# Two attentions in one block: score order, unit order, where the bias is built, and how operands are evacuated

## The chip, the cores and the metric

The kernel runs on one core of one Trainium2 chip. The metric is the device time of one execution in microseconds. A core has TensorE (matmuls, written PE in the profile; its weight loads are a row of their own, PEld), VectorE (DVE), ScalarE (ACT), GpSimd (POOL) and SyncE (SP), from whose queue the DMA transfers are issued.

## The reference, cut to what matters

Two transformer blocks run one after the other on 256 rows of 1024 numbers. The change lies in the first one, which has two attentions side by side:

```python
h = rmsnorm(x, attn_norm_g)
qa, ka, va, qb, kb, vb = split(h @ w_in)            # 512, 128, 128, 512, 512, 512 columns
# grouped: 8 query heads share 2 key heads of 64 columns
qa, ka = apply_axial_rope(rmsnorm(qa, g)), apply_axial_rope(rmsnorm(ka, g))
out_a = softmax(qa @ ka.T / 8) @ va
# differential: 4 heads, each with two score maps (c = 0, 1) of 64 columns, and a bias by distance
s = rmsnorm(qb, g) @ rmsnorm(kb, g).T / 8 + rel_bias[bucket(k - q)]
p = softmax(s)
out_b = rmsnorm((p[c=0] - lam * p[c=1]) @ vb) * 0.8 * g
x = x + concat(out_a, out_b) @ w_out
x = x + square(relu(rmsnorm(x, mlp_norm_g) @ w_up)) @ w_down
```

Everything is float32. The second block (two gated feed-forward layers, an mLSTM, a forgetting attention) is untouched.

## The kernel before, in words

**Weights and operands.** Weights stream through `Stream` (lines 84 to 147): seven raw buffers are loaded ahead from the SP queue (line 108 or 110), then each load is split into two fp32r halves, `hi` by ScalarE (line 133) and the residual `lo` by an engine named per load, VectorE unless a set in `cdef` says GpSimd (line 134). Six pairs of halves can be alive. A product is three matmuls (lines 251 to 253: hi by hi, hi by lo, lo by hi). The activations' own halves come from `gained` (lines 422 to 432) or `to_hl`: TensorE transposes, ScalarE evacuates the high half, VectorE the residual.

**Order.** The program is written in one order, and the framework (`schedule_with_timeline_sim=True`) deals the instructions out to the engines' queues with that order as priority and a clock of its own, so the order on an engine can differ from the program. Each engine then runs its queue in order.

**The opening.** `opening` (lines 322 to 347) computes keys and values of the grouped attention and its queries for both row tiles, with the weights of eight loads; `rope` and `head_norm` follow on VectorE and ScalarE. Accumulators come from three banks (`acc`), everything else from four (`aux`) and from an eighth bank, `flex`, which every fifth `aux()` takes until the differential attention begins.

**The bias.** Line 609 multiplies the bias table by a one-hot matrix, four fp32 matmuls of 32 rows and 512 columns ahead of the opening in the program. Lines 612 and 614 evacuate them, line 617 stores them to DRAM with a pitch of 513, and line 880, behind the opening, reads them back with a pitch of 512, so that each row is shifted by one.

**The units.** After the opening come twelve units: eight grouped ones (row tile, pair of heads, key head) and then four differential ones (row tile, pair of heads). Each has three stages: `scores`, `trans` (TensorE transposes the exponentials), `pvs`. A loop of 14 passes runs the scores of unit i, the transposes of unit i-1 and the products of unit i-2, then one `fill()`. A fill is the next half chunk of the projections kb, qb, vb (four each), or the next block of the output projection (`wout_q`, two for each row tile and each half of its rows), which is queued when the unit that completes its operand is done. `have` draws fills at once where a unit needs a projection that isn't there yet. In a score matmul the contraction has 64 rows, so it uses one half of the array's 128 rows: key head 0 the lower half, key head 1 the upper; for the differential units map c = 0 the lower and c = 1 the upper. Before, one grouped unit's two matmuls lie on one half. An fp32 matmul shows as two records in the trace.

**The end of the block.** `ev_wo` adds to x and calls `gained` for the next layer's operand, whose `opening` starts the MLP.

## Time and profile before

| what | value |
|---|---|
| median of three runs | 1053.79 us (1047.0 to 1056.36) |
| the profiled execution | 1052.49 us |
| its span, first to last instruction | 1050.7 us |
| mean granted TensorE clock | 0.983 of 2.4 GHz |
| moved by DMA | 212.21 MB, 202 GB/s on average |

The profile is of one execution. Times in the trace count from the span's start. A timeline row gives start and length in us, then engine, line, operation, output and inputs, shapes and how many instructions were merged; in brackets stands how long the engine had been idle and what ended that. A table by stretches gives each engine's busy time in a stretch, the granted clock (1.00 is 2.4 GHz, 0.50 is 1.2 GHz), the share of the DMA engines that was taken and GB/s.

### The profile page before, as it was taken

To read this page: it belongs to the slowest core of one execution; us is meant where nothing else is said; L and a number is where in the kernel's file an instruction comes from. 1 tells how busy PE (TensorE), PEld (TensorE's weight loads), DVE (VectorE), ACT (ScalarE), POOL (GpSimd) and SP (SyncE) were. 2 spreads that over 40 slices of the span, in tenths; PEclk is the share of its full clock that TensorE was granted. 3 is DMA by queue.
4 is the path that set the end of the run, shared out by engine and by line. 5 is a ranking of instruction groups with operands and counts; after the bars stand their busy time and mean duration, and the time that the engine had idled before them with its cause. 6 is when DMAs were issued, how large, how long until landed. Compare 5 with 4: busy or idle time off the path is not lost.

```text
span 1050.7 us, 15208 instructions
## 1 busy us (share of the span) xinstructions
PE 1016.8 (97%) x5861; PEld 870.4 (83%) x5861; DVE 721.6 (69%) x1009; ACT 513.3 (49%) x803; POOL 41.4 (4%) x45
## 2 busy tenths in 40 slices
PE   8899899999999999999999989999999989999998
PEld 5678678998888899998879767787788868999987
DVE  5866657889675565668767889875669776665652
ACT  5567457554453455445434645343464535445540
POOL 1131000000000000000010000000010000000000
PEclk7989999999999999999999999999999999999999
DMA  8734237888884566679817577665456545664741
GB/s 305 235 120 143 79 109 248 272 280 272 314 280 145 181 201 200 183 244 371 284 58 225 179 238 240 205 193 158 134 188 209 201 140 183 218 230 152 263 158 41
DMA packets 104651, 212.21 MB, mean 202 GB/s; under 512 B 7933, under 2 KB 14937, under 8 KB 104578
## 3 DMA queue, kind: packets, MB, share of 16 engines
q1 hardware_dynamic: 104578, 211.24, 60.9%
q8 instruction: 46, 0.75, 0.3%
q14 instruction: 27, 0.22, 0.1%
HBM read 209.11 MB, written 2.10 MB: 201 GB/s over the span
## 4 chain that ended last, share of the span: by engine, by line
PE 71%; DVE 12%; DMA 9%; issue 4%; ACT 2%; SPq 0%; POOL 0%; DVEq 0%; ACTq 0%
PE acc L251 13%; PE acc L252 13%; PE acc L253 12%; DMA raw<-in_w_ada_dram 9%; DVE lo L134 7%; PE acc L312 3%; PE flex L251 3%; PE acc L313 3%; PE flex L253 3%; PE acc L311 3%; PE flex L252 3%; PE flex L311 1%; PE flex L312 1%; PE flex L313 1%; PE aux L375 1%
## 5 line engine op out<-in xcount | busy, mean ns | idle before, releaser
L134 DVE TENSOR_TENSOR lo<-raw,hi 128x1024 fp32r<-128x1024 f32 (+1 forms) x290 | 340.3, 1196 | 68.7 <-ACT hi L133 67.1
L133 ACT ACTIVATE hi<-raw 128x1024 fp32r<-128x1024 f32 (+1 forms) x297 | 301.6, 1027 | 136.7 <-PE acc L253 52.3
L312 PE MATMUL acc<-X,lo 128*128 128x256 f32 x624 | 175.6, 281 | 1.5 <-DVE lo L134 1.5
L311 PE MATMUL acc<-X,hi 128*128 128x256 f32 x624 | 175.8, 282 | 0.0
L313 PE MATMUL acc<-X,hi 128*128 128x256 f32 x624 | 175.4, 281 | 0.0
L472 DVE SCALAR_TENSOR_TENSOR mod<-raw,sc,mod 128x1024 f32<-128x1024 f32 x72 | 92.7, 1288 | 108.3 <-DMA raw<-in_w_ada_dram 108.0
L251 PE MATMUL acc<-hi,X 128*128 128x512 f32 (+1 forms) x320 | 130.7, 410 | 10.8 <-DVE z L1246 4.1
L253 PE MATMUL acc<-hi,X 128*128 128x512 f32 (+1 forms) x320 | 127.5, 401 | 1.2 <-DVE X L380 1.2
L252 PE MATMUL acc<-lo,X 128*128 128x512 f32 (+1 forms) x320 | 127.7, 401 | 0.9 <-DVE lo L134 0.9
L312 PEld LDWEIGHTS acc<-X,lo 128*128 128x128 f32 x624 | 118.2, 189 | 2.1 <-DVE lo L134 1.9
L311 PEld LDWEIGHTS acc<-X,hi 128*128 128x128 f32 x624 | 118.3, 190 | 0.2
L313 PEld LDWEIGHTS acc<-X,hi 128*128 128x128 f32 x624 | 118.1, 189 | 0.3
L251 PEld LDWEIGHTS acc<-hi,X 128*128 128x128 f32 x320 | 61.8, 194 | 30.1 <-DVE z L1246 5.0
L253 PEld LDWEIGHTS acc<-hi,X 128*128 128x128 f32 x320 | 61.8, 193 | 17.8 <-DVE X L432 1.9
L252 PEld LDWEIGHTS acc<-lo,X 128*128 128x128 f32 x320 | 62.0, 194 | 13.6 <-DVE lo L134 1.5
L252 PE MATMUL acc<-lo,U 128*128 128x512 f32 x174 | 68.3, 394 | 1.1 <-DVE lo L134 1.1
L253 PE MATMUL acc<-hi,U 128*128 128x512 f32 x174 | 68.4, 395 | 0.0
L251 PE MATMUL acc<-hi,U 128*128 128x512 f32 x174 | 68.0, 395 | 0.0
L311 PE MATMUL flex<-X,hi 128*128 128x256 f32 x208 | 58.6, 281 | 0.0
L312 PE MATMUL flex<-X,lo 128*128 128x256 f32 x208 | 58.5, 281 | 0.0
L313 PE MATMUL flex<-X,hi 128*128 128x256 f32 x208 | 58.5, 281 | 0.0
L252 PEld LDWEIGHTS acc<-lo,U 128*128 128x128 f32 x174 | 32.7, 188 | 9.1 <-DVE lo L134 1.4
(427 smaller groups left out, 1705.1 us busy)
## 6 DMA issues: line engine op xcount, KB each, us to landing
raw<-in_ffn_w_in_dram SPq DMA_DIRECT2D x80, 512.0 KB, 4.9
raw<-in_w_ada_dram SPq DMA_DIRECT2D x72, 512.0 KB, 4.8
raw<-in_w_mix_dram SPq DMA_DIRECT2D x64, 512.0 KB, 4.5
raw<-in_ffn_w_out_dram SPq DMA_DIRECT2D x44, 512.0 KB, 5.8
raw<-in_w_up_dram SPq DMA_DIRECT2D x32, 512.0 KB, 4.8
raw<-in_w_down_dram SPq DMA_DIRECT2D x32, 512.0 KB, 5.5
raw<-in_w_in_dram SPq DMA_DIRECT2D x16, 512.0 KB, 5.6
raw<-in_w_out_dram SPq DMA_DIRECT2D x16, 512.0 KB, 3.6
```

The lines of the kernel that those rows point to most:

```text
L133: nc.scalar.activation(hi[:, :, :n], r[:, :, :n], AF.Copy)
L134: getattr(nc, eng).tensor_tensor(lo[:, :, :n], r[:, :, :n], hi[:, :, :n].bitcast(F32), ALU.subtract)
L251: nc.tensor.matmul(ps[:, c0:n], h, hi[:, j, c0:n], start=f, stop=False)
L252: nc.tensor.matmul(ps[:, c0:n], h, lo[:, j, c0:n], start=False, stop=False)
L253: nc.tensor.matmul(ps[:, c0:n], l, hi[:, j, c0:n], start=False, stop=z)
L311: nc.tensor.matmul(ps, h, xh, start=first, stop=False, skip_group_check=True)
L312: nc.tensor.matmul(ps, l, xh, start=False, stop=False, skip_group_check=True)
L313: nc.tensor.matmul(ps, h, xl, start=False, stop=last, skip_group_check=True)
L375: nc.tensor.transpose(ps[:, b * P : (b + 1) * P], src[:, b * P : (b + 1) * P], ident)
L472: nc.vector.scalar_tensor_tensor(v, r.rearrange("p a c -> p (a c)"), sc[:, k : k + 1], v, ALU.mult, ALU.add)
```

## The change

Six things change, all in the first block:

- `gained`: VectorE multiplies all 512 columns of a bank by the gain into an SBUF tile, ScalarE copies that as the high half, VectorE subtracts for the residual. Before, each engine did this in four pieces of 128 columns.
- The projections qb and vb no longer name GpSimd for their residuals; VectorE makes all of them.
- The bias is built behind the opening. The table is cut into three bf16 parts stacked on 96 rows, and the one-hot matrix is bf16, three times, so that one bf16 matmul of 96 rows per head replaces the fp32 one. Store and reload keep their form; the reload is issued after the first two fills.
- A grouped pair (key heads 0 and 1) issues its four score matmuls together, in turns between the halves of the array, when its first unit is reached; the second unit finds its bank filled. A differential unit issues its four in turns between the maps.
- The units run as four grouped ones, then differential and grouped in turns: d0, g4, d1, g5, d2, g6, d3, g7.
- `wout_q` starts an accumulator with whichever half of the rows comes first, since for the second row tile that is now the differential one.

```diff
     onehot[bucket, np.arange(512)] = 1.0
+    onehot = np.concatenate([(onehot.view(np.uint32) >> 16).astype(np.uint16).view(np.float32)] * 3, axis=0)
...
     def gained(t, half, g, X):
...
-        for b in range(4):
-            v, gain = ps[:, b * P : (b + 1) * P], cols[:, g + 4 * half + b : g + 4 * half + b + 1]
-            nc.scalar.activation(dh[:, b], v, AF.Identity, bias=0.0, scale=gain)
-            nc.vector.scalar_tensor_tensor(dl[:, b], v, gain, dh[:, b].bitcast(F32), ALU.mult, ALU.subtract)
+        v = s512("xg").rearrange("p (b q) -> p b q", b=4)
+        gain = cols[:, g + 4 * half : g + 4 * half + 4].unsqueeze(2).to_broadcast([P, 4, P])
+        nc.vector.tensor_tensor(v, ps.rearrange("p (b q) -> p b q", b=4), gain, ALU.mult)
+        nc.scalar.activation(dh, v, AF.Copy)
+        nc.vector.tensor_tensor(dl, v, dh.bitcast(F32), ALU.subtract)
...
-        "kava": (512, 256, ()), "qa": (0, 512, ()), "kb": (1280, 512, ()), "qb": (768, 512, (0, 1, 2, 3)),
-        "vb": (1792, 512, (1, 2, 3)),
+        "kava": (512, 256, ()), "qa": (0, 512, ()), "kb": (1280, 512, ()), "qb": (768, 512, ()),
+        "vb": (1792, 512, ()),
...
-    oh = s512("oh")[:32]
-    nc.sync.dma_start(oh, a["onehot"])
...
         def scores(u):
             qt, jp, g = u
...
-            ps = aux()
-            for i in range(2):
-                nc.tensor.matmul(
-                    ps[:, i * S : (i + 1) * S], qaT[g * 64 : (g + 1) * 64, 2 * jp + i, qt * P : (qt + 1) * P],
-                    kaT[g * 64 : (g + 1) * 64, :], start=True, stop=True,
-                )
+            if g == 0:
+                for w in range(2):
+                    sc2[w] = aux()
+                for i in range(2):
+                    for w in range(2):
+                        nc.tensor.matmul(
+                            sc2[w][:, i * S : (i + 1) * S], qaT[w * 64 : (w + 1) * 64, 2 * jp + i, qt * P : (qt + 1) * P],
+                            kaT[w * 64 : (w + 1) * 64, :], start=True, stop=True,
+                        )
+            ps = sc2.pop(g)
...
-            for c in range(2):
-                ps = aux()
-                for i in range(2):
-                    h = 2 * hp + i
+            pss = [aux(), aux()]
+            for i in range(2):
+                h = 2 * hp + i
+                for c in range(2):
                     nc.tensor.matmul(
-                        ps[:, i * S : (i + 1) * S], qbT[c * 64 : (c + 1) * 64, h, qt * P : (qt + 1) * P],
+                        pss[c][:, i * S : (i + 1) * S], qbT[c * 64 : (c + 1) * 64, h, qt * P : (qt + 1) * P],
                         kbT[c * 64 : (c + 1) * 64, h, :], start=True, stop=True,
                     )
+            for c in range(2):
+                ps = pss[c]
...
     opening(xv, it_c["kava"], 256, ev_kava, it_c["qa"], 512, ev_qa)
-    for qt in range(2):
-        o = 255 - P * qt
-        nc.sync.dma_start(bias[:, :, qt, :], tr[:, :, o : o + S])
+    oh = ph.tile([96, S], F32, name="oh")
+    nc.sync.dma_start(oh, a["onehot"])
+    rbp, rbb, rbr = ph.tile([96, 4], BF16, name="rbp"), ph.tile([32, 4], BF16, name="rbb"), ph.tile([32, 4], F32, name="rbr")
+    nc.vector.tensor_copy(rbp[0:32], rb)
+    nc.vector.tensor_tensor(rbr, rb, rbp[0:32], ALU.subtract)
+    nc.vector.tensor_copy(rbb, rbr)
+    nc.vector.tensor_copy(rbp[32:64], rbb)
+    nc.vector.tensor_tensor(rbr, rbr, rbb, ALU.subtract)
+    nc.vector.tensor_copy(rbp[64:96], rbr)
+    bias = bigt([P, 4, 2, S], F32, "bias")
+    for h in range(4):
+        psb = aux()
+        nc.tensor.matmul(psb, rbp[:, h : h + 1].to_broadcast([96, P]), oh.bitcast(BF16), start=True, stop=True)
...
     def wout_q(t, kh):
         for n in range(2):
-            if kh == 0:
+            first = (n, t) not in wo_ps
+            if first:
                 wo_ps[n, t] = acc()
             st.need(it_wo[kh][n])
-            block(wo_ps[n, t], *mv, 4 * kh, it_wo[kh][n], t, 512, kh == 0, kh == 1)
-            if kh == 1:
+            block(wo_ps[n, t], *mv, 4 * kh, it_wo[kh][n], t, 512, first, not first)
+            if not first:
...
-    units = [(gqa_stages, u, (), 0) for u in gqa_units] + [(diff_stages, u, ("kb", "qb"), 1) for u in diff_units]
+    ga_, df_ = [(gqa_stages, u, (), 0) for u in gqa_units], [(diff_stages, u, ("kb", "qb"), 1) for u in diff_units]
+    units = ga_[:4] + [v for pair in zip(df_, ga_[4:]) for v in pair]
...
     fill(2)
     flush()
+    for qt in range(2):
+        o = 255 - P * qt
+        nc.sync.dma_start(bias[:, :, qt, :], tr[:, :, o : o + S])
```

## Rows read from the trace of the kernel before

**Rows 1.** Page: busy us, share of span, instructions.

```profile
PE 1016.8 (97%) x5861; PEld 870.4 (83%) x5861; DVE 721.6 (69%) x1009; ACT 513.3 (49%) x803; POOL 41.4 (4%) x45
```

**Rows 2.** Stretches: length; busy us (instructions) per engine; PEclk; DMA share; GB/s.

```profile
9.00:23.00 14.00, 13.86 (x34) 7.99 (x34) 8.91 (x24) 8.27 (x22) 0.55 (x1) 0.53 1.02 376
...
45.00:57.00 12.00, 7.29 (x28) 4.19 (x27) 9.10 (x28) 6.65 (x20) 0.00 (x0) 0.68 0.14 46
57.00:122.70 65.70, 65.69 (x354) 51.97 (x352) 43.64 (x78) 41.67 (x90) 12.67 (x5) 0.98 0.42 137
122.70:131.20 8.50, 4.12 (x18) 3.63 (x19) 5.17 (x12) 3.85 (x11) 1.02 (x1) 0.80 0.00 0
131.20:153.00 21.80, 20.08 (x94) 15.15 (x93) 10.01 (x20) 10.02 (x21) 2.00 (x3) 1.00 0.24 76
153.00:372.00 219.00, 218.64 (x1296) 192.56 (x1295) 159.42 (x173) 116.19 (x158) 3.00 (x4) 1.00 0.73 246
```

**Rows 3.** Stretches, line 609 alone: PE, PEld, PEclk, DMA share, GB/s.

```profile
9.00:23.00 14.00, 5.69 (x6) 1.49 (x6) 0.53 1.02 376
23.00:45.00 22.00, 1.12 (x2) 0.29 (x2) 1.00 0.95 285
```

**Rows 4.** TensorE's timeline: grouped units (761) alone, a differential unit (824).

```profile
54.64 2.07 PE L761 MATMUL aux<-kaT,qaT 64*128 64x256 f32 x4
...
64.79 1.13 PE L761 MATMUL aux<-kaT,qaT 64*128 64x256 f32 x4
...
106.09 1.14 PE L824 MATMUL aux<-kbT,qbT 64*128 64x256 f32 x8
```

**Rows 5.** One microsecond in which the clock rises; columns as rows 2.

```profile
22.00:23.00 1.00, 1.00 (x3) 0.19 (x1) 0.00 (x0) 0.27 (x1) 0.00 (x0) 0.98 1.06 389
```

**Rows 6.** SP queue, 0 to 60 us, and landing times of the loads.

```profile
4.94 4.15 SPq L110 DMA_DIRECT2D raw<-in_w_in_dram  x6
...
DMA to landing us min/median/max: 5.2/5.5/7.0
```

**Rows 7.** ScalarE's timeline: the seventh load's split.

```profile
25.99 1.06 ACT L133 ACTIVATE hi<-raw 128x1024 fp32r<-128x1024 f32 x1 [2.15 <-issue]
```

**Rows 8.** SP queue: the bias stored and read back.

```profile
24.96 0.37 SPq L617 DMA_DIRECT2D toep<-bias  x1
...
33.96 0.92 SPq L880 DMA_DIRECT2D bias<-toep  x2
```

**Rows 9.** VectorE and GpSimd timelines, 33 to 46 us; GpSimd's splits to 165 us.

```profile
33.52 0.29 DVE L673 TENSOR_TENSOR m<-kn,rc 128x128 f32<-128x128 f32 x1
...
37.75 1.23 DVE L134 TENSOR_TENSOR lo<-raw,hi 128x1024 fp32r<-128x1024 f32 x1
...
39.61 2.13 DVE L673 TENSOR_TENSOR m<-kn,rc 128x128 f32<-128x128 f32 x1
41.66 2.55 DVE L679 TENSOR_TENSOR m<-kn,rs 128x64 f32<-128x64 f32 x2
...
39.19 4.80 POOL L134 TENSOR_TENSOR lo<-raw,hi 128x1024 fp32r<-128x1024 f32 x2 [27.26 <-ACT hi L133]
...
L134 POOL TENSOR_TENSOR lo<-raw,hi 128x1024 fp32r<-128x1024 f32 x7 | 17.5, 2515 | 56.4 <-ACT hi L133 56.2
```

**Rows 10.** Chain of waits, 100 to 132 us: start, length, what.

```profile
118.58 2.09 ACT s L836 x8
...
122.03 1.20 DVE s L829 x2
123.23 1.19 DVE nm L833 x2
```

**Rows 11.** TensorE's timeline in the tail.

```profile
127.08 0.66 PE L375 MATMUL aux<-ident,ob 128*128 128x128 f32 x4 [4.40 <-DVE ob L451]
```

**Rows 12.** Groups to 165 us: busy us, mean ns; the rest is idle time.

```profile
L431 ACT ACTIVATE X<-aux,cols 128x128 fp32r<-128x128 f32 x28 | 9.2, 362 | 4.0 <-DVE X L432 2.5 <-PE aux L427 1.5
L432 DVE SCALAR_TENSOR_TENSOR X<-aux,cols,X 128x128 fp32r<-128x128 f32 x28 | 9.0, 344 | 3.0 <-ACT X L431 2.9
```

More of the change, by code (lines that the diff above doesn't have):

```diff
@@ L603, in body @@
         nc.vector.tensor_scalar(e1[:, t : t + 1], v, EPS, None, ALU.mult)
-    bias = bigt([P, 4, 2, S], F32, "bias")
-    for h in range(4):
-        psb = aux()
-        nc.tensor.matmul(psb, rb[:, h : h + 1].to_broadcast([32, P]), oh, start=True, stop=True)
-        v = bias[:, h].rearrange("p t k -> p (t k)")
-        if h % 2:
-            nc.vector.tensor_copy(v, psb)
-        else:
-            nc.scalar.activation(v, psb, AF.Copy)
-    pitch = 512
-    toep = dram.tile([4, P * (pitch + 1)], F32, name="toep")
-    nc.sync.dma_start(toep.rearrange("h (p j) -> p h j", j=pitch + 1)[:, :, :512], bias.rearrange("p h t k -> p h (t k)"))
-    tr = toep[:, : P * pitch].rearrange("h (p j) -> p h j", j=pitch)
     gq8 = const.tile([P, 9], F32, name="gq8")
@@ L752, in gqa @@
     def gqa():
-        pv, rec, ex, exT = {}, {}, {}, {}
+        pv, rec, ex, exT, sc2 = {}, {}, {}, {}, {}
         def scores(u):
@@ L877, in body @@
     opening(xv, it_c["kava"], 256, ev_kava, it_c["qa"], 512, ev_qa)
-    for qt in range(2):
-        o = 255 - P * qt
-        nc.sync.dma_start(bias[:, :, qt, :], tr[:, :, o : o + S])
+    oh = ph.tile([96, S], F32, name="oh")
[11 more added lines that the diff above has]
+        nc.tensor.matmul(psb, rbp[:, h : h + 1].to_broadcast([96, P]), oh.bitcast(BF16), start=True, stop=True)
+        v = bias[:, h].rearrange("p t k -> p (t k)")
+        if h % 2:
+            nc.vector.tensor_copy(v, psb)
+        else:
+            nc.scalar.activation(v, psb, AF.Copy)
+    pitch = 512
+    toep = dram.tile([4, P * (pitch + 1)], F32, name="toep")
+    nc.sync.dma_start(toep.rearrange("h (p j) -> p h j", j=pitch + 1)[:, :, :512], bias.rearrange("p h t k -> p h (t k)"))
+    tr = toep[:, : P * pitch].rearrange("h (p j) -> p h j", j=pitch)
     sc = const.tile([P, 8], F32, name="sc")
```

## The prediction

> **What bounds the kernel now.** I read four views in this order: the engine totals, a table by stretches, the chain of waits, and timelines of the stretches that look bad. In the totals TensorE is busy 97% of the span and VectorE 69% [rows 1], so TensorE sets the time wherever it has no hole. The table shows where it has holes or runs slowly [rows 2]. From 57 to 122.7 us it is busy 65.69 of 65.70 us at a granted clock of 0.98, and from 153 to 372 us it is as full: there only fewer TensorE instructions help. Three stretches of the first block are not like that. From 9 to 23 us TensorE is busy throughout, but the clock is 0.53, which is the 1.2 GHz level nearly all the time, while the DMA engines are fully taken (1.02). From 45 to 57 us it is busy 7.29 of 12 us, at 0.68. From 122.7 to 131.2 us it is busy 4.12 of 8.5 us, at 0.80. All that the change touches lies before 161 us. What follows 153 us keeps its code, its numbers of banks and its seven load buffers, so I take it to move forward as a whole by whatever the front saves.
>
> The profiled execution took 1052.49 us for a span of 1050.7 us, 1.3 us under the median of the three runs (1053.79). I make the sum against 1052.5 us. The three runs spread over 9 us, so I take about 1%, some 10.5 us, as what a measurement can tell from no change.
>
> **Part 1, the bias matmuls leave the opening.** They take 5.69 us of TensorE between 9 and 23 us and 1.12 us after that, 6.81 us for eight records [rows 3], and they stand in the middle of the opening's own matmuls, in a stretch without a hole. Afterwards there are four bf16 matmuls of 512 columns. The nearest rows are the score records, 0.27 us each at 2.4 GHz and 0.52 us at 1.2 GHz [rows 4], so four cost 1.1 to 2.1 us; I take 1 us and book it as a loss, since it may fall where TensorE is full. A second gain is the clock: it comes back to 2.4 GHz at about 23 us [rows 5], after fourteen busy microseconds. If it comes back earlier, each microsecond brought forward gives back half a microsecond; if holes open where the bias matmuls were, it comes later. What can take this gain away is the data. The opening needs eight weight loads; the last of them is issued by 9.1 us, and loads land 5.2 to 7.0 us after issue [rows 6], thus by 14 to 16 us. The seventh load's split runs on ScalarE only at 25.99 us [rows 7], ten microseconds after its data, because ScalarE stands in order behind the bias evacuations. So the data is not the limit after 16 us, while before that TensorE would now wait for it. Bounds: nearly all waits, 1 us; all 6.8 us and 2.5 us of clock, 9.3 us. I take 6.5 us, near the row that shows the data early.
>
> The store of the bias and its two reloads move from 25 and 34 us to behind the opening; from the store's issue to the reload's it is 9 us [rows 8]. The reloads now stand on SP behind the weight loads that the first half of the key projection asks for, and while they wait for the store every later weight load waits behind them. The bias is read first by the first differential unit, now the fifth unit: four passes after the first scores, each a half chunk (2.8 us) and a unit (1.8 us), thus some 18 us. Store and reload together I estimate at 17 us, the 9 us and nearly as much again. I cost this at nothing, covered by the 18 us; without the cover it costs the missing part, up to 5 us, once.
>
> **Part 2, splits from GpSimd to VectorE.** Seven residuals of 1024 columns take 17.5 us on GpSimd, and VectorE needs 1.23 us for one, so VectorE gets 8.6 us more work [rows 9]. But VectorE loses time beside them: the rotary multiply of 128 columns takes 0.29 us at 33.5 us and 2.13 us at 39.6 us, and the two half as wide that follow take 2.55 us together, exactly while GpSimd splits (39.19 to 43.99 us) [rows 9]. With 0.29 us each as an upper bound for the three, that is about 4 us on the chain that leads to the first queries; against it stand two splits at 1.23 us, a net gain of about 1.5 us there. The larger effect is what hangs on it. From 45 to 57 us all accumulation banks are held by results that VectorE has not read, so the key projection cannot go on. What TensorE really does in these 12 us, taken at 2.4 GHz, is fifteen transposes and three score units, 3.8 us; so about 8 us are lost, and 1.2 us more from 57 to 59.7 us at 1.2 GHz. With VectorE four microseconds earlier and the opening shorter, the first queries are ready while the key projection still has work. Bounds: 0 (the hole only moves) to 9 us; I take 6 us. The other five splits, 6 us of VectorE, fall in 57 to 122.7 us, where VectorE is busy 43.64 of 65.70 us [rows 2] and TensorE covers them.
>
> **Part 3, the alternating scores.** One grouped unit alone is four records in 1.06 us at 2.4 GHz and 2.0 us at 1.2 GHz; a differential unit is eight records in the same 1.07 us [rows 4]. So two matmuls on different halves of the rows run side by side, at the price of one. The first pair of grouped units and three of four differential units already ran that way, because the framework's order had put them so. What is left are six single grouped units, three pairs, 3 x 1.06 = 3.2 us, in stretches where TensorE is full. Bounds 0 and 4 us; I take 3.2 us.
>
> **Part 4, the order of units and the tail.** The fillers are twelve half chunks and eight output blocks. Today there is always one until pass 12 of 14. In the new order the first differential unit (fifth) draws two at once, and by my count the queue is empty in passes 10 and 11, with the last differential and grouped unit still to come. There TensorE has about 6 us of units beside a chain of 14 us: additions and maxima 2.4, exponentials 2.09, combination 1.3, the normalization and its transposes some 5, plus transposes and products [rows 10]. Against that, the first half of the output projection for the second row tile now ends the phase, and the chain of the last differential unit is partly covered by the last grouped one. Today's tail loses 4.40 us waiting for the normalized output [rows 11], about 2 us at the low clock after it and 2 us of small holes up to 153 us. Bounds: 7 us worse to 6 us better. I take 1.5 us better, because the next layer's opening can start on the first row tile in these holes, as it already does today.
>
> **Part 5, the wide evacuation.** Thirty-two ScalarE and thirty-two VectorE instructions of 0.36 and 0.34 us (28 of each in [rows 12], four more of each read the flex bank) become eight of 512 columns on ScalarE and sixteen on VectorE, at some 0.6 us each (the additions in rows 10 are 0.60 us of 512 columns). ScalarE saves 7 us; VectorE is even. The kernel's first operand comes perhaps 0.5 us later, three steps of 0.6 us instead of two of 0.35 us. I take 0, bounds -1 and +1.5.
>
> **Sum.** 6.5 + 6 + 3.2 + 1.5 - 1 = 16.2 us; 1052.5 - 16.2 = 1036.3, so 1036 us. Its own range is 1028 to 1043.
>
> **Rivals.** (a) The opening is bound by its data. For it speaks the DMA share of 1.02 from 9 to 23 us; against it the late seventh split. Part 1 then gives 1 us instead of 6.5: 1042 us. (b) The fillers run out. TensorE is idle in the tail for the differential chain, 14 - 6 = 8 us, while part 4's gain of 1.5 us goes: 1052.5 - 16.2 + 1.5 + 7 = 1045 us. For it the count of fillers; against it the next opening's matmuls. (c) The change does not do what it says: the framework deals the instructions out by its own clock and alternates no more than now. Then 3.2 us are missing, and with the order of the late units unchanged the 1.5 us too: 1041 us. (d) Slower: the score banks. The second bank of a grouped pair is written with the first and read a unit later, with a differential unit, which takes two banks, between; with one for transposes all four are taken. Each of the eight late units then waits until a bank is read. One such wait is a unit's additions, maxima and exponentials, 2.4 + 2.1 = 4.5 us [rows 10]; eight make 36 us, and where a filler of 2.8 us lies beside it (about four) 11 us are covered: 1052.5 - 16.2 + 25 = 1061 us. It decides from 2 us for each of the eight waits. For it speaks the count of banks; against it that from 96 to 122 us, with the same two banks for a differential unit, TensorE has no hole.
>
> The Trainium skill speaks for (d): TensorEngine Tiling says under Restrictions and Gotchas that splitting the rows raises the pressure on PSUM, since different row tiles write different banks, and under Performance Considerations that the evacuation does not get faster with it. The rows of before neither show such a wait nor exclude it; by that rule the time would be that of (d).
>
> **How the numbers follow.** Forecast 0.52, (a) 0.16, (b) 0.14, (c) 0.10, (d) 0.08. The bound of 1% is 1043.3 us on one side and 1064.3 us on the other. Faster: nearly all of the forecast (0.49), most of (a) (0.10) and (c) (0.08), a third of (b) (0.05), 0.72 together. Slower: some of (d) and mishaps like a late bias, 0.07. Same: 0.21. The range goes from 1024 us, where parts 1 and 2 reach their upper bounds, to 1049 us, which holds (a), (c) and most of (b).
>
> **What would show it.** Right: the opening's last matmul before 40 us instead of 45; no hole over 2 us around the first scores and no VectorE multiply over 1 us; every score stretch with eight records in about 1.07 us; the phase end (now 153 us) near 137 us; the rest equally long. Wrong: holes in the weight matmuls of the opening that end on a load (a); several microseconds before the last normalized output (b); score stretches of four records (c); TensorE waiting on exponentials or maxima for a bank in the last eight units (d). A stretch after 160 us that changes by more than 2 us would refute that the rest only shifts.

## The result, and the profile after

The change made the kernel slower: 1063.91 us median (1060.27 to 1066.62, six runs) against 1052.06 us, a ratio of 1.0114 with a 95% interval of 1.0075 to 1.0154. The forecast was 1036 us and the range ended at 1049. The profiled execution has a span of 1064.8 us, 14.1 us more than before.

The engine totals of after, beside [rows 1]:

```profile
PE 1018.1 (96%) x5857; PEld 876.9 (82%) x5857; DVE 722.6 (68%) x1006; ACT 508.2 (48%) x779; POOL 23.0 (2%) x38
```

TensorE is busy only 1.3 us longer, VectorE 1.0 us, ScalarE and GpSimd less. So nearly all of the 14 us is time in which TensorE stands idle; how much of its busy time is matmuls at a lower clock, these totals don't tell. The table by stretches, with the bounds of [rows 2] and one stretch more, says where (length; busy us per engine; granted clock; DMA share; GB/s):

```profile
9.00:23.00 14.00, 12.57 (x73) 11.33 (x74) 12.50 (x36) 11.18 (x23) 1.11 (x2) 0.88 1.03 369
...
37.00:45.00 8.00, 4.03 (x24) 2.37 (x23) 7.57 (x21) 5.82 (x17) 0.00 (x0) 0.91 0.79 222
...
45.00:57.00 12.00, 12.00 (x55) 9.59 (x55) 6.35 (x11) 7.44 (x13) 0.00 (x0) 0.77 0.61 171
57.00:122.70 65.70, 55.71 (x267) 43.35 (x266) 39.16 (x72) 32.47 (x73) 1.01 (x1) 0.90 0.37 125
...
131.20:153.00 21.80, 16.09 (x68) 13.62 (x68) 8.26 (x17) 8.10 (x20) 1.01 (x1) 0.69 0.00 1
```

The front is better, as forecast: from 9 to 23 us the clock is 0.88 instead of 0.53 and 73 matmul records stand there instead of 34. The first exponential of a grouped unit starts at 43.7 us instead of 53.3, so 9.6 us were won there. The hole ahead of it has not closed, though, it has only moved: from 45 to 57 us TensorE is now full, but from 37 to 45 us it is busy 4.03 of 8 us. Then it turns. From 57 to 122.7 us TensorE had no hole and a clock of 0.98; now it misses 10 of 65.7 us and runs at 0.90. From 131.2 to 153 us it is busy 16.09 of 21.8 us at 0.69. The last ReLU in the opening of the MLP's up projection, which I use as the mark of the attentions' end and call the end of the first block, starts at 182.7 us instead of 173.8.

What TensorE waited for between 44 and 165 us (engine, tile and line, what it waited for: us in total, times, longest):

```profile
PE aux L377 <- DVE ob L454: 5.7, 2, 3.8
PE aux L844 <- DVE s L836: 3.1, 1, 3.1
PE aux L773 <- ACT e L762: 3.0, 1, 3.0
PE acc L786 <- ACT eT L775: 2.4, 1, 2.4
PE flex L857 <- ACT aT L846: 1.9, 3, 0.7
PE acc L253 <- ACT qbT L716: 1.8, 1, 1.8
PE aux L815 <- ACT e L762: 1.7, 1, 1.7
```

Before, the same view held one wait over a microsecond from 57 to 160 us, that on `ob` [rows 11]. Two of the seven lines are waits for a bank. In the last a differential unit's scores (line 815) can't be written before the exponentials (line 762) have read what is in the bank; in the sixth a projection (line 253) can't start before ScalarE has read the transposed queries (line 716) out of an accumulator bank. The others are waits for an attention's own chain. Four of all these waits stand in the tail, here with length, operation and, in brackets, the idle time ahead:

```profile
114.70 0.66 PE L377 MATMUL aux<-ident,ob 128*128 128x128 f32 x4 [3.78 <-DVE ob L454]
...
125.00 1.13 PE L751 MATMUL aux<-kaT,qaT 64*128 64x256 f32 x8
...
128.90 1.14 PE L815 MATMUL aux<-kbT,qbT 64*128 64x256 f32 x8 [1.74 <-ACT e L762]
...
135.61 0.55 PE L844 MATMUL aux<-ident,s 128*128 128x128 f32 x2 [3.13 <-DVE s L836]
...
143.69 1.11 PE L377 MATMUL aux<-ident,ob 128*128 128x128 f32 x4 [1.89 <-DVE ob L454]
```

Eight records in 1.13 us for two grouped units (line 751) are the pairs, as designed. Behind three of these four stands a low clock, which the prediction charged to no new wait: part 4 names 2 us at the low clock behind the old wait on `ob`, but rival (b) counts idle time alone. The same stretch in steps of four microseconds; the column to read is the granted clock, the third from the end:

```profile
116.00:120.00 4.00, 3.87 (x9) 3.09 (x10) 0.75 (x1) 0.08 (x1) 0.00 (x0) 0.50 0.00 0
120.00:124.00 4.00, 4.00 (x14) 3.18 (x14) 0.69 (x1) 0.72 (x2) 0.00 (x0) 0.74 0.00 0
...
136.00:140.00 4.00, 3.31 (x16) 2.91 (x14) 0.00 (x0) 1.08 (x2) 0.00 (x0) 0.50 0.00 0
140.00:144.00 4.00, 2.11 (x11) 1.93 (x11) 1.91 (x4) 0.60 (x1) 1.01 (x1) 0.50 0.00 0
144.00:148.00 4.00, 4.00 (x14) 3.19 (x13) 1.67 (x3) 1.28 (x2) 0.00 (x0) 0.50 0.01 4
```

After the wait on `ob` TensorE is full from 116 us on, but at 0.50, the 1.2 GHz level: the 24 matmuls of the output projection that start at 116.13 us take 8.5 us instead of the 5.74 us that the same 24 take at 1.00 in a run below (e9). After the wait on `s` the clock is 0.50 for twelve microseconds. These stalls are paid twice, once as idle time and once as slow matmuls behind them.

That can be counted. For each kernel of this study I cut the time from the first grouped exponential to that last ReLU into one-microsecond stretches and added up TensorE's idle time, and its busy time multiplied by one minus the granted clock ("lost to the clock"). What is left is the work at full clock. The last column is from the read-out of the second block's gates (the ScalarE instruction that writes `gt`) to the last merge, with mLSTM and forgetting attention between. All in us:

| kernel | length | idle | lost to the clock | rest | second block's mixing |
|---|---|---|---|---|---|
| before | 120.5 | 6.8 | 4.5 | 109.2 | 273.9 |
| after | 139.0 | 18.2 | 15.0 | 105.8 | 278.1 |
| e1, old unit order | 121.1 | 10.4 | 4.6 | 106.1 | 272.1 |
| e2, only unit order | 136.0 | 15.8 | 11.8 | 108.5 | 280.1 |
| e3, single scores | 133.6 | 13.8 | 10.3 | 109.5 | 276.6 |
| e4, row-tile order | 138.9 | 16.7 | 13.1 | 109.1 | 271.8 |
| e5, only bias | 121.9 | 6.8 | 6.2 | 108.9 | 273.0 |
| e6, only splits | 120.6 | 7.7 | 3.3 | 109.7 | 272.5 |
| e7, only scores | 126.5 | 9.6 | 9.5 | 107.4 | 271.8 |
| e8, early draw | 132.4 | 13.6 | 10.8 | 108.0 | 273.8 |
| e9, stalls kept busy | 134.8 | 12.9 | 7.4 | 114.5 | 271.6 |
| e10, the same, old order | 126.9 | 11.4 | 4.5 | 111.0 | 271.6 |
| e11, old order, single scores | 121.1 | 6.9 | 5.5 | 108.7 | 271.3 |

Each row is one execution, and executions of one kernel spread over several microseconds (e8's take 1044.94 to 1056.60 us). The stretch of unchanged code between that ReLU and the gates is 381.1 to 383.9 us long in twelve of the kernels and 386.9 in e8, so a difference of 3 us in the length of a stretch can be chance.

The rest is 105.8 to 109.7 us in all kernels without added work; the lengths differ by idle time and by what the clock takes after it. From before to after the stretch grew by 18.5 us: 11.4 us idle and 10.5 us of clock, against 3.4 us of work saved. With the 9.6 us won ahead of it the first block ends 8.9 us later; the other 5 us of the span lie behind that mark, 4.2 of them in the second block's mixing (last column). Counted the same way from the first matmul to the first exponential, the 9.6 us are clock and work: the loss to the clock is 1.4 us instead of 7.9 and the rest 33.2 instead of 36.3, while the idle time, with the hole in it, is 8.1 instead of 8.2.

### The profile page after: what moved, and what is told of

Same layout as the page of the kernel before. It is cut to its first block, busy times and chain, and to the rows that moved or that the text cites. A ratio compares the mean times of both kernels' runs of the same rounds, so it can differ in the third digit from the quotient of the medians.

```text
span 1064.8 us, 15169 instructions
## 1 busy us (share of the span) xinstructions
PE 1018.1 (96%) x5857; PEld 876.9 (82%) x5857; DVE 722.6 (68%) x1006; ACT 508.2 (48%) x779; POOL 23.0 (2%) x38
## 4 chain that ended last, share of the span: by engine, by line
PE 57%; issue 21%; DVE 5%; DMA 2%; ACT 1%; POOL 0%; DVEq 0%; ACTq 0%; POOLq 0%
PE acc L253 9%; PE acc L255 8%; PE acc L254 8%; PE acc L314 6%; PE acc L315 6%; PE acc L313 6%; DVE lo L136 3%; PE flex L255 3%; PE flex L253 3%; PE flex L254 3%; DMA raw<-in_w_ada_dram 2%; PE flex L313 2%; PE flex L315 2%; PE flex L314 2%; PE aux L377 1%
## 5 line engine op out<-in xcount | busy, mean ns | idle before, releaser
L136 DVE TENSOR_TENSOR lo<-raw,hi 128x1024 fp32r<-128x1024 f32 (+1 forms) x297 | 345.9, 1185 | 70.5 <-ACT hi L135 68.9
L253 PEld LDWEIGHTS acc<-hi,X 128*128 128x128 f32 x320 | 63.0, 197 | 23.3 <-ACT X L381 2.3
L255 PEld LDWEIGHTS acc<-hi,X 128*128 128x128 f32 x320 | 62.8, 196 | 15.0 <-DVE X L382 1.7
L136 DVE TENSOR_TENSOR wbig<-raw,wbig 128x1024 fp32r<-128x1024 f32 x22 | 26.8, 1224 | 19.1 <-ACT wbig L135 18.5
```

The source lines that it names most:

```text
L136: getattr(nc, eng).tensor_tensor(lo[:, :, :n], r[:, :, :n], hi[:, :, :n].bitcast(F32), ALU.subtract)
L253: nc.tensor.matmul(ps[:, c0:n], h, hi[:, j, c0:n], start=f, stop=False)
L255: nc.tensor.matmul(ps[:, c0:n], l, hi[:, j, c0:n], start=False, stop=z)
```

## Experiments

**The order of the units alone, both ways.** e1 is the changed kernel with the old order, e2 the kernel before with the new one.

```diff
# e1 (e2 the other way round, in the kernel before)
-    units = ga_[:4] + [v for pair in zip(df_, ga_[4:]) for v in pair]
+    units = [(gqa_stages, u, (), 0) for u in gqa_units] + [(diff_stages, u, ("kb", "qb"), 1) for u in diff_units]
```

> The changed kernel with the old order of units (eight grouped, then four differential); pairs, bias, splits and evacuation stay changed. Theory U (the unit order loses it: both halves of the second row tile's output projection wait for the last pair, so nothing is left to cover the last chains, about 22 us between the first differential unit and the end of the phase, while everything before is 10 to 15 us faster): 1037 to 1043 us, and the mixing layer, whose queues are dealt out as before, is as long as before. Theory B (the score banks of a pair, held for a unit): only part comes back, 1046 to 1056 us. Theory O (the other parts bring nothing): 1050 us or more.

> The kernel before with the new order of units alone (and the accumulator start that it needs). Theory U: the loss without the gains, 1066 to 1080 us. Theory B: no pair holds a bank here, so 1049 to 1057 us.

e1 took 1040.29 us (ratio to before 0.9905, 0.9871 to 0.9939), e2 1073.55 us (1.0224, 1.0186 to 1.0262). The order costs 23 us in either company, 22.9 us from before to e2 and 23.6 us from e1 to after, so it doesn't depend on the other parts. By the marks it is 15.9 and 17.4 us in the first block. In both pairs about 6 us more come in the second block's mixing, 273.9 to 280.1 and 272.1 to 278.1, whose code and order in the program are the same in all these kernels. Everything else together, e1 against before, is 10 us faster.

**Pairs in the new order.** e3 is the changed kernel with each grouped unit issuing its own scores again.

```diff
-            if g == 0:
...
-            ps = sc2.pop(g)
+            ps = aux()
+            for i in range(2):
+                nc.tensor.matmul(
+                    ps[:, i * S : (i + 1) * S], qaT[g * 64 : (g + 1) * 64, 2 * jp + i, qt * P : (qt + 1) * P],
...
```

> The changed kernel with each grouped unit issuing its own two score matmuls again; the unit order stays new. Theory U: still slow, 1062 to 1072 us (up to 3 us above the changed kernel for the lost pairing). Theory B: the banks are free again, 1052 us or less.

1057.96 us (1.0066, 1.0039 to 1.0094), between the two: both theories missed. The pairs cost 6 us here, where the prediction had them save 3.2 us. They do save that much work (rest 105.8 us with, 109.5 without), but idle time and clock take 9 us more. TensorE's waits in e3 show no wait of line 810, the differential scores, for a bank any more, and the late wait on `s` shrinks from 3.13 us:

```profile
131.00 0.44 PE L839 MATMUL aux<-ident,s 128*128 128x128 f32 x2 [0.86 <-DVE s L831]
```

So rival (d) exists, but as one wait for a score bank of 1.74 us instead of eight waits and 25 us. Nor is it the whole 6 us: the transposes of the first `ob` start at 111.74 us in e3 and at 114.70 in after, so half of the 5.9 us between the two ends of the first block is lost ahead of that wait. After waits there 2.37 us for an `eT` at 66 us, where e3 waits 0.63; how the pairs bring that about was not followed up. The rule of the Trainium skill that stood with it in the prediction (TensorEngine Tiling, Restrictions and Gotchas: row tiles press on PSUM) holds here in kind, and is far from deciding.

**Row tile by row tile.** In the new order both differential units of the second row tile stand near the end, so both halves of its output projection come last. e4 places the units so that one row tile is finished first.

```diff
-    units = ga_[:4] + [v for pair in zip(df_, ga_[4:]) for v in pair]
+    units = ga_[:4] + df_[:2] + ga_[4:] + df_[2:]
```

> The changed kernel with its units ordered by row tile: four grouped, two differential, four grouped, two differential. The differential units still come as early as in the changed kernel and draw the projections early, but the first half of the second row tile's output projection is free before the last two units. Theory U: nearly all comes back, 1036 to 1046 us. Rival E (the early draw of the projections is what costs): 1055 us or more.

1056.85 us (1.0054, 1.0017 to 1.0091). The theory that the late halves make the loss falls: the first block ends at 182.0 us, like after's 182.7. Nearly the whole gain against after is in the second block, where the mixing takes 271.8 us instead of 278.1. What e4 shares with after is that the first differential unit is the fifth, so the early draw remained.

**The early draw alone.** e8 keeps e1's order of units but makes the projections of the differential attention as early as the new order has to.

```diff
+            if i == 4 and j == 0:
+                have("kb", "qb")
+            if i == 6 and j == 2:
+                have("vb")
```

> The changed kernel with the old order of units (1040.3), but with the projections of the differential units drawn as early as the new order draws them (keys and queries at pass 4, values at pass 6), so that the late passes have as few blocks to fill with as in the changed kernel, while the order of the units stays the old one. If the fillers run out because they are drawn early, most of the 23.6 us comes back in the first block: 1050 to 1060. If it is the order of the units itself (differential chains beside grouped ones, exposed alone at the end, or bank waits among them), the early draw costs little: 1038 to 1044.

1051.05 us (1.0018, 0.9991 to 1.0045), 10.8 us over e1; its first block ends 10.0 us later. Of the two places where this shows, the first is the draw itself. A projection waits 1.77 us for the accumulator bank that ScalarE reads the transposed queries from; the same wait, 1.77 us long, stands in after, e2, e3, e4 and e9, and in none of the kernels that draw late. And after a wait of 1.45 us on a normalized projection (`kn`) the clock falls. The second is the time after it, with fewer blocks left to fill (TensorE's timeline at the two waits, then the clock):

```profile
73.18 0.50 PE L253 MATMUL acc<-hi,X 128*128 128x512 f32 x1 [1.77 <-ACT qbT L716]
...
80.66 0.66 PE L715 MATMUL acc<-ident,kn 128*128 128x128 f32 x4 [1.45 <-DVE kn L454]
```

```profile
80.00:84.00 4.00, 3.34 (x17) 2.67 (x17) 2.25 (x6) 2.55 (x7) 0.00 (x0) 0.79 0.70 243
84.00:88.00 4.00, 4.00 (x11) 2.76 (x11) 1.69 (x5) 0.93 (x4) 0.00 (x0) 0.50 0.00 1
...
108.00:112.00 4.00, 1.56 (x7) 1.13 (x7) 3.22 (x7) 2.20 (x8) 0.00 (x0) 0.71 0.01 4
112.00:116.00 4.00, 4.00 (x20) 3.25 (x19) 1.96 (x5) 1.06 (x3) 0.00 (x0) 0.50 0.00 0
```

Counted as in the table, 60 to 92 us loses 6.6 us against 1.6 in e1, 3.4 of them to the clock, and the tail (92 to 135 us, in e1 92 to 125) 13.4 us against 7.8. The wait on `kn` is not the draw's own: e1 has it too, with 1.64 us, but the clock stays at 1.00 there. So the early draw explains 10 of the 17.4 us of the first block. The pairs in the new order are another 5.9 us by the same mark (176.8 us in e3). That leaves 1.5 us for the rest of the order, if the two add up; that they do was not tried. Without the grouped pairs the order costs the first block 15.9 us (e2) or 13.0 (e3 against e11, 176.8 and 163.8), so the pairs' share of the 17.4 us may be as small as 1.5 to 4.4 us, with more left for the rest.

**Each of the other parts alone.** e5 moves the bias, e6 only drops `(0, 1, 2, 3)` and `(1, 2, 3)` from the entries `"qb"` and `"vb"` of `cdef`, e7 only has the scores alternate.

```diff
# e5
-    oh = s512("oh")[:32]
-    nc.sync.dma_start(oh, a["onehot"])
...
+    oh = ph.tile([96, S], F32, name="oh")
+    nc.sync.dma_start(oh, a["onehot"])
...
+        nc.tensor.matmul(psb, rbp[:, h : h + 1].to_broadcast([96, P]), oh.bitcast(BF16), start=True, stop=True)
```

```diff
# e7 (grouped units; the differential ones issue i outside c inside)
+            if g == 0:
+
+                for w in range(2):
+                    sc2[w] = aux()
+                for i in range(2):
+                    for w in range(2):
...
+            ps = sc2.pop(g)
```

> The kernel before, with the relative-bias block alone moved behind the opening (and built from bf16 parts). As the prediction priced it, this part alone is worth 6.5 us of the opening: 1043 to 1047 against about 1051. Rival: the four f32 bias products and the evacuations are not the last thing that the opening waits for, so that their removal alone gives 2 us or less and only the two parts together give the 8 to 10 us by which the changed kernel with the old order was ahead.

> The kernel before, with GpSimd's shares of the splits of the diff weights alone given back to VectorE. As the prediction priced it, this part (with the wide evacuation) is worth 6 us: 1043 to 1047. Rival: the weights are split well ahead of their matmuls and VectorE only gets fuller: within 2 us of before or slower.

> The kernel before, in its old order of units, with the scores alone changed to alternate between the row halves. The prediction's third part: 3 us faster (1047 to 1049). The theory of bank waits: the second bank of a pair is held through the first one's chain, 1054 to 1060. A third reading, from the run of the changed kernel with single scores in the new order (the pairing cost 6 us there): in the old order there are fillers, so that waits on banks cost little and gains are filled as well: within 2 us of before.

e5: 1040.76 us against 1050.13 (0.9898, 0.9864 to 0.9933). One part of six gives the whole gain of e1. e6: 1048.36 us (0.9982, 0.9961 to 1.0004), within the rival's 2 us. e7: 1054.33 us (1.0050, 1.0021 to 1.0080), at the edge of the bank theory's range.

The opening from 9 to 23 us and the hole ahead of the first exponential, first in e5:

```profile
9.00:23.00 14.00, 12.57 (x73) 10.91 (x72) 12.68 (x45) 10.86 (x29) 0.56 (x1) 0.89 1.04 370
...
37.00:45.00 8.00, 3.72 (x19) 1.97 (x19) 7.47 (x22) 4.99 (x15) 0.00 (x0) 0.86 0.33 119
```

and in e6:

```profile
9.00:23.00 14.00, 14.00 (x34) 7.59 (x32) 8.27 (x23) 7.98 (x20) 0.56 (x1) 0.50 1.04 382
23.00:33.00 10.00, 10.00 (x45) 7.82 (x45) 5.07 (x16) 4.64 (x11) 0.00 (x0) 0.71 0.73 167
...
45.00:57.00 12.00, 8.94 (x46) 6.54 (x45) 9.64 (x28) 5.83 (x18) 0.00 (x0) 0.96 0.28 106
```

With the fp32 bias products in the opening TensorE is full but granted 1.2 GHz until 23 us and longer. Without them it has 1.4 us of holes from 9 to 23 us and 0.89 of the clock. The hole that I laid on VectorE's slow multiplies closes in neither. In e5, where GpSimd still splits, it comes with the first exponential some 8 us earlier (3.72 of 8 us busy), and in e6, where GpSimd doesn't split, it stays, at 8.94 of 12 us busy. The multiplies did change as reasoned. The line of all their records in e5, then in e6 (min/median/max in ns):

```profile
L657 DVE TENSOR_TENSOR m<-kn,rc x2: 292/1246/2199, 23.0 to 30.6; 128x128 f32<-128x128 f32 x2
```

```profile
L673 DVE TENSOR_TENSOR m<-kn,rc x2: 284/288/291, 36.3 to 44.6; 128x128 f32<-128x128 f32 x2
```

The Trainium skill, SBUF — State Buffer, section "SBUF: two separate sides", says that VectorE and GpSimd share a port pair which, where VectorE's instruction has two inputs in SBUF, one of them holds for a whole instruction while the other is fully blocked. The trace agrees, 2.20 us (GpSimd splits from 30.21 to 35.01 us) against 0.29 us. But the time doesn't follow: the first exponential starts at 45.0 us in e5, with the slow multiply, and at 54.1 us in e6, without.

e7 is the plainest case of the clock. Its row of TensorE where it loses most, and the clock behind it:

```profile
95.31 0.66 PE L729 MATMUL acc<-ident,kn 128*128 128x128 f32 x4 [2.92 <-DVE kn L451]
```

```profile
92.00:96.00 4.00, 1.08 (x9) 0.77 (x7) 3.90 (x9) 0.69 (x1) 0.00 (x0) 1.00 0.75 220
96.00:100.00 4.00, 4.00 (x15) 2.93 (x13) 1.50 (x4) 2.78 (x8) 0.00 (x0) 0.54 0.49 174
100.00:104.00 4.00, 4.00 (x9) 2.78 (x10) 1.45 (x3) 0.58 (x4) 0.00 (x0) 0.50 0.00 0
104.00:108.00 4.00, 4.00 (x16) 3.15 (x15) 2.04 (x5) 2.91 (x6) 0.00 (x0) 0.68 0.00 0
```

One wait of 2.92 us on a normalized projection, then 12 us of full work at 0.54, 0.50 and 0.68, worth 5.1 us (4 x 0.46 + 4 x 0.50 + 4 x 0.32). The wait is not for a score bank, and the transposes of `kn` stand where they stood before (95.33 us there, without a wait). It is `kn` that is late, by VectorE's queue. Before, VectorE makes `kn` first and then a multiply for a later layer's modulation (`mod`); in e7 the framework dealt the `mod`, which waits for its own weight load, and two weight splits ahead of `kn`. VectorE's timeline, before and then e7:

```profile
90.92 0.68 DVE L451 TENSOR_TENSOR kn<-acc,rs 128x512 f32<-128x512 f32 x1
...
93.25 1.28 DVE L472 SCALAR_TENSOR_TENSOR mod<-raw,sc,mod 128x1024 f32<-128x1024 f32 x1
```

```profile
90.44 1.29 DVE L472 SCALAR_TENSOR_TENSOR mod<-raw,sc,mod 128x1024 f32<-128x1024 f32 x1 [2.31 <-DMA raw<-in_w_ada_dram]
...
94.57 0.69 DVE L451 TENSOR_TENSOR kn<-acc,rs 128x512 f32<-128x512 f32 x1
```

In e1 and e8 a `mod` stands ahead of the `kn` in question as well, and waits 1.57 and 1.59 us for its load.

e11 asks what the pairs do in the old order with the better opening: e1 without alternating scores.

> The changed kernel with the old order of units and single scores, so that only the bias, the splits and the wide evacuation are changed. Prediction's third part: 3 us slower than with the pairs (1043). Theory of bank waits in any order: 4 to 6 us faster (1034 to 1036). Third reading, from the sums of busy time: pairs save about 3 us of TensorE's busy time everywhere, and what they cost lies in stalls that depend on how the pieces interleave; in this order the pairs were seen to cost no stall, so 1041 to 1044.

1040.01 us (0.9910, 0.9883 to 0.9937), the same as e1. The table repeats the pattern: 2.6 us less work with the pairs, 3.5 us more idle time. The third reading came nearest, but it was wrong too in that the pairs' gain of 3 us doesn't reach the end of the kernel.

**Stalls kept busy.** e9 tests the clock's share. It adds nine useless products of 512 columns to the changed kernel, written to the bank of the transposes that wait and then overwritten. e10 does it in e1, five in the one long stall.

```diff
+    def keep(ps, n):
+        for _ in range(n):
+            nc.tensor.matmul(ps, ident, warm[0][:, 0:2, :].rearrange("p h k -> p (h k)"), start=True, stop=True)
...
         ps = aux()
+        keep(ps, n)
...
+            keep(p2, 3 if u == (1, 1) else 0)
...
-                to_hl(ob, MX, 4, qt, g=gsub)
+                to_hl(ob, MX, 4, qt, g=gsub, n=(4, 2)[qt])
```

> The changed kernel with nine useless products added (128x128 by 512, f32; their results are overwritten), placed in front of transposes for which TensorE waits 3 to 4 us in the first block: four before the wait on ob of row tile 0, three before the wait on s of the last differential unit, two before that of row tile 1. Theory: a stall costs its own length and, behind it, as much again at 1.2 GHz; products in the stall keep the clock, so that the stretches 116 to 122 and 136 to 150 run at 1.0 and the time falls by 4 to 8 us, to 1056 to 1060. Rival: the stalls alone cost, whatever the clock; then nine products of about 0.9 us are idle time filled at best and late work at worst: 1063 to 1068.

> The changed kernel with the old order of units and five useless products of the same kind in its one long stall (5.1 us on ob of row tile 0, after which 116 to 122 ran at 0.50 to 0.70). Theory: 2 to 3 us below that kernel's 1040.3, 1037 to 1039. Rival: no gain or a loss of up to 2 us, 1040 to 1043.

e9: 1052.40 us against 1049.46 (1.0030, 1.0011 to 1.0048), 11.5 us less than after by the medians and more than the theory's 4 to 8 us, with more work. TensorE's timeline at the first of the stalls, and the clock behind it:

```profile
109.30 3.60 PE L376 MATMUL aux<-kbT,ident 128*128 128x512 f32 x8
...
114.08 0.66 PE L384 MATMUL aux<-ident,ob 128*128 128x128 f32 x4 [0.35 <-DVE ob L461]
```

```profile
116.00:120.00 4.00, 4.00 (x20) 3.27 (x19) 0.94 (x2) 0.25 (x1) 0.00 (x0) 1.00 0.00 0
120.00:124.00 4.00, 3.78 (x26) 2.75 (x24) 2.50 (x5) 1.11 (x3) 0.00 (x0) 1.00 0.00 0
...
140.00:144.00 4.00, 4.00 (x13) 3.19 (x12) 1.47 (x3) 1.28 (x2) 0.00 (x0) 0.50 0.02 4
```

The four products (eight records, 3.60 us) stand in the wait, and the output projection behind it starts at 1.00 and takes 5.74 us instead of 8.50. From 128 to 136 us the clock holds as well. At 136 us, ahead of the last `ob`, the framework dealt the two products elsewhere, a wait of 2.65 us stayed, and the clock fell as before. In the table the loss to the clock is halved, from 15.0 to 7.4 us, and the first block ends 4.2 us earlier, as the theory had it. The other 7 us came from behind it, 6.5 by the second block's mixing, and were not forecast. The Trainium skill, TensorE: Matmul & The Clock Gate, section "HAM oscillation — how this bites in real kernels", describes a kernel whose TensorE loses its clock in each wait for a DMA and starts the matmuls behind at the lower one; the rows of e7 and e9 agree, those of e3 in the last section don't.

e10: 1041.44 us (0.9914, 0.9891 to 0.9938), no gain over e1's 1040.29. Its profile doesn't test the point: the five products took 4.46 us from 115.18 us on, and behind them 3.98 us of waiting for `ob` were left, so the stall was not filled but moved. The framework dealt the products between the two halves of the third differential unit's transposes, and ScalarE's copy of these (119.89 us) stands ahead of the squares from which `ob` is normalized (120.39 us, in e1 115.36). An earlier wait, on `kn`, took 3.25 us in it and 1.64 us in e1's profile, though the queue is the same up to there: the `mod` ahead of it waited 3.20 us for its weight load instead of 1.57.

**The second block.** In the ten kernels of the table whose mixing takes 271.3 to 273.9 us and in the three where it takes 276.6 to 280.1, the code of the second block is the same. The queues are not: the framework dealt the instructions of the mixing layer out in another order in after, e2 and e3. After has there one stall that e9 doesn't have, with the same sequel (TensorE's timeline in the mLSTM, then the clock):

```profile
665.30 1.08 PE L1270 MATMUL aux<-ident,z 128*128 128x128 f32 x4 [3.20 <-DVE z L454]
```

```profile
660.00:670.00 10.00, 6.78 (x27) 5.01 (x26) 9.23 (x14) 2.97 (x5) 0.00 (x0) 0.74 0.72 228
670.00:680.00 10.00, 10.00 (x41) 8.07 (x40) 6.73 (x13) 4.80 (x8) 0.00 (x0) 0.92 0.51 149
```

In e9 the wait at the corresponding place is 1.69 us and the clock stays at 1.00:

```profile
658.30 0.50 PE L253 MATMUL acc<-hi,X 128*128 128x512 f32 x1 [1.69 <-DVE z L1273]
```

```profile
654.00:664.00 10.00, 8.31 (x40) 6.51 (x39) 9.88 (x17) 4.54 (x9) 0.00 (x0) 1.00 0.85 258
```

Which of the changes tips the framework's order there was not found; e4 and e9 tip it back by edits that have nothing to do with the second block.

## Why the prediction was wrong

**The step that failed: part 4, the order of units and the tail.** It put the new order at 1.5 us better, between 7 worse and 6 better; it is 23 us worse. The mechanism stood in the text, as rival (b): the draw of two projections at once, the queue empty in passes 10 and 11, a chain of 14 us with 6 us of units beside it. It was priced at 8 us of idle time and 0.14. The rows bear its count out, for from 124.6 to 145.6 us TensorE has no block of a projection left. The price was wrong, in four ways that overlap: the early draw also costs at once (e8: 5.0 of 10.6 us between 60 and 92 us, 3.4 of them clock); the stalls together are paid again at 1.2 GHz (10.5 us of clock beside 11.4 us of idle time); the pairs cost 6 us in this order (e3); and the second block was dealt out anew (6 us). Its sum, moreover, adds 7 us for the 8 it names. "The next layer's opening can start on the first row tile in these holes" did not cover it: with 0.69 of the clock and 16.09 of 21.8 us busy there was little of it.

**"What follows 153 us ... to move forward as a whole"** failed by its own test: of the stretches after 160 us, the mixing changed by 4.2 us, over the 2 us set as the bound. The stretch between the two, from the last ReLU to the gates, is equal (383.9 and 383.4 us).

**Part 1** had the right sign and was too small: 6.5 us forecast, upper bound 9.3; alone it gives 9.4 us by the medians (e5; 7.0 to 14.3 by the interval), 8.3 us at the first exponential and 6.9 us at the end of the first block. The mis-sized term was the clock, with 2.5 us in the upper bound: up to the first exponential the loss to the clock falls from 7.9 us before to 2.1 in e5, the work at full clock only from 36.3 to 33.5. I had read the 0.53 of the opening as a level that comes back a few microseconds earlier; without the fp32 products it is 0.89 from 9 to 23 us. Rival (a), the data, isn't seen in the 1.4 us of holes there: none ends on a weight load, after's is for the input rows `x` (1.61 us) and e5's for a split on ScalarE (1.13 us). The late bias cost nothing that shows: in after VectorE's waits from 44 to 165 us hold none for it, and in e1 a split waits 3.65 us for the bias's reload while TensorE is full.

**Part 2** was credited with 6 us and gives between 4.1 us gained and 0.4 lost (e6's interval); in the first block nothing, where its mark is 174.7 us against 173.8. The observation (multiplies stretched by GpSimd) was right, the step from it to the hole of 45 to 57 us was wrong. That hole stands ahead of the first exponential in before, e5, e6 and after alike, and moves with it: the lower bound of part 2, "the hole only moves". What keeps it open was not tested. With the bias out of the opening the faster chain may be worth some 2 us: the first exponential starts at 42.7 us in e11, with parts 2 and 5, and at 45.0 in e5.

**Part 3**: the pairs save 1.8 to 3.7 us of TensorE work in each of the three comparisons, near the 3.2 us forecast. None of it reached the end: 4 us slower alone (e7), nothing with the better opening (e11 against e1), 6 us slower in the new order (e3). "In stretches where TensorE is full" was true of the old queue, and the queues change with the part, as VectorE's did in e7.

**Part 5** was not measured alone. With part 2 it separates e5 from e11, 1040.76 and 1040.01 us: nothing that can be told.

By the runs the sum is -9.4 (part 1), about 0 (parts 2, 3 and 5 in the old order), +23 (the order, which includes the pairs' 6 us in it), thus 13.6 us slower; the profiled spans say 14.1, the medians 11.9. The lower end of the forecast's range, 1024 us, takes the upper bounds of all five parts; with those of parts 1 and 2 alone it would be 1030.5.

The best version is the change without the new order, e1 at 1040.29 us, 0.9905 of before; e5 and e11 are not distinguishable from it. Moving the bias out of the opening is the part to keep.

## What to carry to other kernels

Price a new stall on TensorE between its length and twice that, for the matmuls behind it, and look in the rows after today's stalls for what the clock does; the new order's 11.4 us more of idle time came with 10.5 us more of clock. Before a wait is laid on the instruction that ends it, look what stood ahead of that one in its engine's queue: here a wait on a normalization was a weight load's. Compare a hole by what it stands in front of, not by fixed times, or one that moved looks closed. Before work is ordered earlier, count what it leaves for later: a queue of fillers spent early leaves the last chain bare, and waiting for the drawn work is a stall of its own. Where a framework deals out the queues, nothing "only shifts": compare a stretch with unchanged code before crediting or charging the change with it.

## What was not expected of the hardware and the framework

Useless matmuls made the kernel's first block faster: nine products, with which the rest in the table is 8.7 us longer, brought 7.6 us of clock and 5.3 us of idle time back, 4.2 us net. A stall of 2.92 us was followed by 12 us of full work at 0.50 to 0.68. But the length of a wait alone doesn't tell whether the clock falls: after 1.45 us on a `kn` in e8 it fell, after 1.64 us on one in e1 it stayed. A wait of 2.85 us in e3, with the clock around it:

```profile
93.31 0.66 PE L377 MATMUL aux<-ident,oa 128*128 128x128 f32 x4 [2.85 <-DVE oa L787]
```

```profile
92.00:96.00 4.00, 2.69 (x21) 2.15 (x22) 3.75 (x6) 1.92 (x4) 0.00 (x0) 1.00 0.97 331
96.00:100.00 4.00, 4.00 (x21) 3.34 (x20) 2.54 (x7) 2.38 (x9) 0.00 (x0) 1.00 0.54 176
```

It is as long as e7's, and the clock stays at 1.00. Why it falls after the one and not after the other these runs don't settle; a price for a single stall therefore has both ends, its length and twice that. In the opening the clock stayed at 0.50 to 0.53 from 9 to 23 us while TensorE was full with fp32 products of 32 rows among its matmuls, and was 0.88 to 0.89 without them, with 1.4 us of holes.
